# The merge of a two-layer encoder trunk, computed by token with 512 weight columns per product

## The chip, the cores and the metric

The kernel runs on one core of a Trainium2 chip. The metric is the device time of one execution in microseconds. The core has five engines that run side by side: TensorE (PE, matrix products; its weight loads are listed as PEld), VectorE (DVE), ScalarE (ACT), GpSimd (POOL) and SyncE (SP). SP and POOL also issue DMAs.

## What is computed

The reference is a trunk of two layers over 256 tokens of width 1024. A layer normalizes its input, projects it (18688 columns in all), runs three token mixers A, B and C in parallel, and merges them:

```python
for l in range(DEPTH):                      # 2 layers
    h = rmsnorm(x, norm_g[l])
    proj = h @ w_in[l]                      # inputs of all mixers, gates, merge logits
    y_a = hgrn2_mixer(...) * silu(a_g)      # (256, 1024)
    y_b = retention_mixer(...) * silu(b_g)  # (256, 2048)
    y_c = rwkv7_mixer(...) * silu(c_g)      # (256, 1024)
    gates = sigmoid(merge.reshape(b, t, 3, D_MODEL))
    mixed = (gates[:, :, 0] * (y_a @ w_branch_a[l])
             + gates[:, :, 1] * (y_b @ w_branch_b[l])
             + gates[:, :, 2] * (y_c @ w_branch_c[l]))
    x = x + mixed @ w_out[l]
return rmsnorm(x, final_norm_g)
```

All arrays are float32. The merge is the part from `gates` to `x + mixed @ w_out`.

## The kernel before

**Two steps of building.** The kernel first records every operation of all engines (`Plan.note`, L274) with the operations that it depends on and a price (`Plan.cost`, L313). `Plan.order` (L372) then plays the engines against each other with these prices: each engine takes, among the operations whose inputs are there, the one with the lowest rank (60 ns times its number in the record, less the length of the work that hangs on it, `Plan.rank`, L444). `Plan.issue` (L448) emits the instructions in that order; so every instruction of the trace has line L453. Which engine runs what next is thus fixed by the prices and the recorded dependences. `Plan.parts` (L227) gives the parts of a tile that an operation touches, in pieces of 16 columns by 32 partitions. A DMA is priced with a time on the issuing queue, a transfer time by its bytes, and a time to landing.

**Weights.** `load_w` (L527) brings a block of 1024 rows by 256 columns as two halves of 512 KB. Each goes into a raw buffer `w_in` by an SP DMA; ScalarE casts it to `w_hi` (float32r), VectorE subtracts to get `w_lo`. There are three raw buffers, five `w_hi` and four `w_lo` (`RW`, L30). The five inputs of the A mixer (`CCE`, L29) come over the POOL queue instead: one DMA into `w_hi`, a negated copy by ScalarE, and an accumulating DMA into `w_lo`.

**Products.** Every large product is made of three float32r products (high by high, high by low, low by high) for each of eight k tiles. `feat_mm` (L546) has the weights as the stationary operand, 128 columns at a time, and moves the 256 tokens past them; its output is by feature. `tok_mm` (L556) has 128 tokens stationary and moves 256 weight columns; its output is by token. Either way a block takes 48 products that move 256 columns each. Outputs lie in PSUM banks of 512 float32 per partition, named by tag: two "pj", two "c", two "n", one "s", one "ab" (`BANKS`, L116).

**A layer.** The C mixer is prepared (`c_prep`, `c_solve`) and scanned (`c_scan`) in eight pairs of heads; between them run the A pairs and then the B pairs (`FILL`). Their results go to DRAM (ya, yb, yc). Then comes `tail` (L1110), the merge. For each branch m (A, B with two halves of rows, C) and each of four blocks b of 256 columns: a gate product into "pj", its sigmoid as exp, min, ln, exp on ScalarE and VectorE into a tile `t_g` (three buffers, TG), the branch product into two "c" banks, a multiplication, and an addition to the sum `t_acc`. Outputs are by feature, as the output projection needs its stationary operand. With the last branch the sum is cast to `m_hi` and subtracted to `m_lo`. The output projection ("wo") then makes four blocks of 256 columns by token; each is added to x, and the squares are summed for the next norm. `load_y` (L1100) fetches a mixer's result when its branch begins. `norm_T` (L593) makes the next layer's h; `final_norm` (L1156) ends the last layer. Nothing but the planned order parts the merge from the scans: its gate products need h alone, so they may run while the scans do.

In the trace tiles carry the names of their places: "ab_vg_t" is `t_g`, "ab_kq_t" and "ab_c_t" are the sum, "c_wa_t" and "c_qm_t" are `m_hi` and `m_lo`, "c_bd_t" is x, "c_y_t" the squares, "c_W_t" their sums. The branch products read "ab_ex_t" (A), "c_Z_t" (B) and "c_rkvg_t" (C).

Of the kernel before, what the change touches and what calls it, by code (L numbers as in the profile page):

```python
# [19 lines left out]
D = 1024  # L20
T = 256
# [3 lines left out]
TOK = ("ai", "bv", "wo")  # L25
# [38 lines left out]
def _blocks():  # L64
# [8 lines left out]
    for p in range(4):  # L73
        r.append((("bq", p), "w_in", 0, [(5120 + 256 * p, 256)]))
        r.append((("bk", p), "w_in", 0, [(6144 + 256 * p, 256)]))
        for h in (2 * p, 2 * p + 1):
            r.append((("bv", h), "w_in", 0, [(7168 + 256 * h, 256)]))
            r.append((("bg", h), "w_in", 0, [(9216 + 256 * h, 256)]))
    for m in range(3):
        for b in range(4):  # L80
            c = 256 * b
            r.append((("mg", m, b), "w_in", 0, [(15616 + 1024 * m + c, 256)]))
            for n, w, r0 in ((("wa", "w_branch_a", 0),), (("wb0", "w_branch_b", 0), ("wb1", "w_branch_b", 1024)),
                             (("wc", "w_branch_c", 0),))[m]:
                r.append(((n, b), w, r0, [(c, 256)]))
    for b in range(4):
        r.append((("wo", b), "w_out", 0, [(256 * b, 256)]))
# [3 lines left out]
for _i, _b in enumerate(_blocks()):  # L91
    BK[_b[0]] = _i
assert len(BK) == NBLK
# [28 lines left out]
class Plan:  # L122
# [3 lines left out]
    def __init__(self, ctx, tc, some):  # L126
# [4 lines left out]
        self.homes, self.base, self.top, self.place, self.turn, self.psum, self.ndram, self.cache = {}, {}, 0, {}, {}, {}, 0, {}  # L131
        self.last, self.readers, self.bank, self.fill = {}, {}, {}, {}
        self.width, self.tenant, self.before = dict(HOMES), {}, {}
        self.width.update({f"w_{k}{i}": 1024 for k, m in RW.items() for i in range(m)})
        for n, k in BANKS:
            for i in range(k):
                t = self.pp.tile([128, 512], F32, name=f"{n}{i}")[:, :]
                self.psum[n, i] = t
                self.base[t.tensor.name] = (None, f"{n}{i}")
# [3 lines left out]
    def home(self, n, era, dt):  # L143
        old = self.tenant.get(n)
        if old is None or self.tiles[old][1] != era:
            k, w = len(self.tiles), self.width[n]
            if old is not None:
                top, size = self.tiles[old][3], 4 * (w // 16 + 2)
                self.before[k] = {p for g in range(top, top + size) for p in [self.last.get(g, -1)] + self.readers.get(g, [])} - {-1}
            self.tiles.append((n, era, dt, self.top, bass.AP(tensor=self.some.tensor, offset=k << 20, ap=[[w, 128], [1, w]]), w))  # L150
            self.top += 4 * (w // 16 + 2)
# [3 lines left out]
    def real(self, ap):  # L155
# [3 lines left out]
        if k not in self.made:  # L159
            n, era, dt, _, _, w = self.tiles[k]  # L160
# [47 lines left out]
    def dram(self):  # L208
        plan = self

        class Dram:
            def tile(self, shape, dt, name, tag=None):
                plan.ndram += 1
                t = plan.dp.tile(shape, dt, name=f"{name}_{plan.ndram}")[:]
                plan.base[t.tensor.name] = (plan.top, 0)
                plan.top += int(np.prod(shape)) // 32 + 1
# [10 lines left out]
    def parts(self, ap):  # L227

        off = int(ap.offset)
        if ap.tensor.name == self.some.tensor.name:  # L230
            if off < 1 << 20:
                return ()
            _, _, _, base, _, w = self.tiles[off >> 20]
            off &= (1 << 20) - 1
        else:
            b = self.base.get(ap.tensor.name)
            if b is None:
                return ()
            base, w = b
            if base is None:  # L240
                return w
        dims = tuple((int(s), int(c)) for s, c in ap.ap)
        key = (base, off, dims)
        r = self.cache.get(key)
        if r is None:
            if w:
                p, c = divmod(off, w)
                ix = np.array([c])
                for s, n in dims[1:]:
                    if s:  # L250
                        ix = (ix[:, None] + s * np.arange(n)).ravel()
                ix = np.unique(ix // 16)
                r = [base + 4 * int(i) + q for q in range(p // 32, (p + dims[0][1] - 1) // 32 + 1) for i in ix]
            else:
                ix = np.array([off])
                for s, n in dims:
                    if s:
                        ix = np.unique((ix[:, None] + s * np.arange(n)).ravel())
                r = [base + int(i) for i in np.unique(ix // 32)]
            self.cache[key] = r  # L260
        return r
# [12 lines left out]
    def note(self, eng, op, args, kw):  # L274
# [4 lines left out]
        pred, true, rd, wr, fresh = set(), set(), [], [], False  # L279
        for a, w in aps:  # L280
            p = self.parts(a)
            if isinstance(p, str):
                if p in self.bank:
                    pred.add(self.bank[p])
                self.bank[p] = n
            else:
                (wr if w else rd).extend(p)
                if w and (op == "copy_predicated" or "accum_op" in kw):
                    rd.extend(p)
        last, readers = self.last, self.readers  # L290
        for g in rd:
            if g in last:
                true.add(last[g])
        for g in wr:
            if g in last:
                pred.add(last[g])
                pred.update(readers.get(g, ()))
            else:
                fresh = True
        if fresh and out.tensor.name == self.some.tensor.name:  # L300
            pred |= self.before.get(int(out.offset) >> 20, set())
        for g in rd:
            readers.setdefault(g, []).append(n)
        for g in wr:
            last[g] = n
            readers[g] = []
# [6 lines left out]
    def cost(self, eng, op, out, ins, args, kw):  # L313
# [3 lines left out]
        def psum(a):  # L317
            return self.base.get(a.tensor.name, (0,))[0] is None

        both = False  # L320
        if op == "dma_start":
# [50 lines left out]
    def order(self):  # L372
# [26 lines left out]
        use, slow = {}, {0: False}  # L399

# [6 lines left out]
        for _ in range(N):  # L407
# [13 lines left out]
            if e == "tensor":  # L421
# [3 lines left out]
                while x < at + hold:  # L425
# [3 lines left out]
                    x = y  # L429
            start[n], now[e] = at, at + hold  # L430
            moves = o[1] == "dma_start"
            if moves:
                dma = max(at + (700. if e == "sync" else 1500.), dma) + o[6]
                end = dma + 1100. + HOP
            for s in succ[n]:
# [21 lines left out]
def trunk(ctx: ExitStack, tc, x, wb, pp, lora, cst, gtab, ng, out):  # L457
# [68 lines left out]

    def load_w(l, key):  # L527

        W = []
        for h in range(2):  # L530
            src = wb[2 * (l * NBLK + BK[key]) + h]
            hi, lo = plan.weight("hi"), plan.weight("lo")
            if key[0] in CCE or key in CCE:

                G.dma_start(hi, src)
                S.activation(lo, hi.bitcast(F32), AF.Copy, scale=-1.0)
                G.dma_start(lo, src, accum_op=ALU.add)
            else:
                raw = plan.weight("in")
                SY.dma_start(raw, src)  # L540
                S.copy(hi, raw)
                V.tensor_sub(lo, raw, hi.bitcast(F32))
            W.append((hi, lo))
        return W

# [564 lines left out]
    def tail(l, ya, yb, yc, x_src, early, pool):  # L1110
        acc = [early.tile([128, 2, T], F32, name=f"t_acc{b}") for b in range(4)]
        Y, xs = [], None
        for m in range(3):
            br = ((("wa", 0),), (("wb0", 1), ("wb1", 2)), (("wc", 3),))[m]
            for b in range(4):
                o = proj(l, ("mg", m, b))
                g = early.tile([128, 2, T], F32, tag="t_g", bufs=TG, name="t_g")
                S.activation(g, o, AF.Exp, scale=-1.0)
                sigmoid_of_exp(g)
                if b == 0:  # L1120
                    Y += [load_y(src, early, pool if m else early, n) for src, n in (((ya, 0),), ((yb[:, 0:8], 1), (yb[:, 8:16], 2)), ((yc, 3),))[m]]
                o = [ps.tile([128, 256], F32, tag="c", name="t_o") for f in range(2)]
# [173 lines left out]
```

## Time and profile before

| | |
|---|---|
| median of 3 runs | 1712.34 us (1711.75 to 1714.05) |
| the profiled execution | 1706.83 us |
| its span, first to last instruction | 1705.0 us |
| TensorE busy | 1627.3 us (95%) |
| VectorE busy | 1265.2 us (74%) |
| ScalarE busy | 1131.8 us (66%) |
| mean granted clock of TensorE | 0.987 |

The profile is of one execution. Busy time is the union of an engine's instructions. Products are pipelined: the duration shown for one is longer than the distance to the next, so what one costs in a row of them is read from starts. The granted clock is 1.00 at 2.4 GHz and 0.50 at 1.2 GHz. A plain float32 product is recorded as two passes, each with a weight load of its own.

### The profile page before, as it was taken

The numbers are of one execution on the slowest core, as the hardware profiler recorded it, in microseconds if no ns is written. First come the engines' busy times: TensorE is split into PE (matmuls) and PEld (weight loads), VectorE is DVE, ScalarE is ACT, GpSimd is POOL, SyncE is SP. The second block draws the span as 40 slices with busy tenths as digits, with TensorE's granted clock in tenths as the row PEclk, the third lists the DMA queues.
The fourth block names the chain that finished last, engine by engine and source line by source line (L and its number), as shares of the span: only waits on it lengthen the run. The fifth ranks groups of instructions, "written<-read, shape, count | busy, mean of one in ns | idle before, by whom it ended". The sixth has DMA issues, their size and how long they took to land.

```text
span 1705.0 us, 33613 instructions
## 1 busy us (share of the span) xinstructions
PE 1627.3 (95%) x12960; PEld 1594.7 (94%) x12960; DVE 1265.2 (74%) x2613; ACT 1131.8 (66%) x2196; POOL 132.4 (8%) x216
## 2 busy tenths in 40 slices
PE   6989999999999999999998899999999999999997
PEld 6878999999999999999898799998899999999997
DVE  5598889897777986555557888899967878865554
ACT  5877778775756757545559587878657567665553
POOL 1211121100000000000021111220000000000000
PEclk9999999999999999999989899999999999999999
DMA  7968788645455456565568767885454554565653
GB/s 247 233 159 187 173 179 206 142 146 169 120 159 143 124 164 223 177 198 185 189 201 190 174 146 207 198 189 111 134 181 117 171 137 136 169 209 178 199 183 103
DMA packets 139392, 292.24 MB, mean 171 GB/s; under 512 B 63584, under 2 KB 68064, under 8 KB 138976
## 3 DMA queue, kind: packets, MB, share of 16 engines
q1 hardware_dynamic: 116192, 206.20, 39.9%
q0 software_dynamic: 23040, 83.90, 22.0%
q8 instruction: 102, 1.67, 0.4%
q14 instruction: 58, 0.48, 0.1%
HBM read 271.17 MB, written 14.68 MB: 168 GB/s over the span
## 4 chain that ended last, share of the span: by engine, by line
PE 70%; DVE 8%; DMA 8%; issue 7%; ACT 6%; POOL 1%; SPq 1%; DVEq 0%; POOLq 0%; ACTq 0%
PE pj L453 38%; PE c L453 16%; PE n L453 9%; PE ab L453 5%; DMA w_in<-in_wb_dram 2%; PE s L453 2%; DMA w_hi<-in_wb_dram 2%; DVE c_tq L453 2%; DMA ab_ex<-ab_ex 1%; DVE w_lo L453 1%; DVE ab_e L453 1%; ACT c_ux L453 1%; ACT w_hi L453 1%; SPq L453 1%; DVE ab_p L453 1%
## 5 line engine op out<-in xcount | busy, mean ns | idle before, releaser
L453 PE MATMUL pj<-h_hi,w_hi 128*128 128x256 f32 x1952 | 562.3, 297 | 10.3 <-ACT ab_e L453 3.5
L453 PE MATMUL pj<-h_hi,w_lo 128*128 128x256 f32 x1952 | 558.3, 295 | 1.7 <-DMA w_lo<-in_wb_dram 1.0
L453 PE MATMUL pj<-h_lo,w_hi 128*128 128x256 f32 x1952 | 553.5, 292 | 0.1
L453 DVE TENSOR_TENSOR w_lo<-w_in,w_hi 128x1024 fp32r<-128x1024 f32 x292 | 354.3, 1220 | 178.3 <-PE pj L453 47.9
L453 ACT CAST w_hi<-w_in 128x1024 fp32r<-128x1024 f32 x292 | 305.2, 1049 | 206.9 <-PE pj L453 70.0
L453 PEld LDWEIGHTS pj<-h_hi,w_hi 128*128 128x128 f32 x1952 | 369.9, 193 | 14.9 <-ACT ab_e L453 3.7
L453 PEld LDWEIGHTS pj<-h_hi,w_lo 128*128 128x128 f32 x1952 | 369.0, 193 | 4.1 <-DMA w_lo<-in_wb_dram 1.4
L453 PEld LDWEIGHTS pj<-h_lo,w_hi 128*128 128x128 f32 x1952 | 369.8, 193 | 2.2 <-DVE h_lo L453 0.6
L453 PE MATMUL pj<-w_lo,h_hi 128*128 128x256 f32 x384 | 111.6, 291 | 2.7 <-DMA w_lo<-in_wb_dram 2.7
L453 PE MATMUL pj<-w_hi,h_hi 128*128 128x256 f32 x384 | 112.5, 293 | 1.4 <-ACT ab_ex L453 1.4
L453 PE MATMUL c<-c_Z,c_bd 128*128 128x192 f32 (+1 forms) x512 | 106.3, 309 | 7.6 <-ACT c_bd L453 4.6
L453 PE MATMUL pj<-w_hi,h_lo 128*128 128x256 f32 x384 | 110.5, 288 | 0.0
L453 PE MATMUL c<-c_Z_t,w_hi 128*128 128x256 f32 x512 | 95.7, 284 | 0.0
L453 ACT COPY c_y<-n 128x128 f32<-128x128 f32 (+1 forms) x160 | 61.8, 392 | 45.8 <-PE n L453 43.7
L453 PEld LDWEIGHTS c<-c_Z,c_bd 128*128 128x128 f32 x512 | 80.6, 196 | 10.2 <-ACT c_bd L453 6.6
L453 ACT ACTIVATE w_lo<-w_hi 128x1024 fp32r<-128x1024 f32 x80 | 84.4, 1056 | 7.7 <-DMA w_hi<-in_wb_dram 5.6
L453 POOL DMA_DIRECT2D w_lo<-in_wb_dram x80 | 71.2, 891 | 175.8 <-ACT w_lo L453 76.2
L453 PE MATMUL n<-c_y,c_wa 128*128 128x128 f32 x512 | 81.1, 279 | 2.5 <-ACT c_y L453 1.5
L453 DVE TENSOR_TENSOR c_tq<-c_W,c_M 128x16 f32<-128x16 f32 (+6 forms) x112 | 81.9, 732 | 1.4
L453 PE MATMUL ab<-ab_e 128*128 128x128 f32 x448 | 73.7, 286 | 8.3 <-DVE ab_p L453 2.5
L453 PEld LDWEIGHTS c<-c_Z_t,w_hi 128*128 128x128 f32 x512 | 79.0, 190 | 0.2
L453 PEld LDWEIGHTS pj<-w_lo,h_hi 128*128 128x128 f32 x384 | 73.3, 191 | 3.8 <-DMA w_lo<-in_wb_dram 3.4
(195 smaller groups left out, 3604.9 us busy)
## 6 DMA issues: line engine op xcount, KB each, us to landing
w_in<-in_wb_dram SPq DMA_DIRECT2D x292, 512.0 KB, 3.8
w_hi<-in_wb_dram POOLq DMA_DIRECT2D x80, 512.0 KB, 5.4
w_lo<-in_wb_dram POOLq DMA_DIRECT2D x80, 512.0 KB, 7.1
c_M<-s SPq DMA_DIRECT2D x64, 128.0 KB, 5.0
c_ux<-in_lora_dram SPq DMA_DIRECT2D x16, 256.0 KB, 2.8
ab_e<-in_gtab_dram SPq DMA_DIRECT2D x16, 256.0 KB, 2.7
ab_ex<-ab_ex SPq DMA_DIRECT2D x16, 256.0 KB, 5.5
yb<-ab_e SPq DMA_DIRECT2D x16, 256.0 KB, 4.0
```

The costliest lines, as they stand in the source:

```text
L453: getattr(getattr(self.tc.nc, eng), op)(*map(self.real, args), **{k: self.real(v) for k, v in kw.items()})
```

## The change

The merge's blocks become 512 columns wide (`WIDE`): per branch two instead of four, and two for the output projection. `wide_mm` has 128 tokens of h, y or m stationary and moves 512 weight columns; a pair of PSUM banks, one per 128 tokens, is filled side by side, k tile by k tile, each half block of 512 KB serving two k tiles. Gates and sums are now by token. After the last branch each sum tile (128 tokens by 512 features) is transposed on TensorE in four pieces into an "n" bank, from which `m_hi` and `m_lo` are taken. The weights are packed on the host to match.

The record keeps, for each tile, exact masks of columns (still by 32 partitions) with the operations that last wrote and read them. Prices change: a POOL DMA holds its queue for 550 ns (870 if it accumulates) instead of 1000 and lands later, a queue is taken to have at most eight DMAs in flight, and for plain float32 products the width of the stationary operand counts in place of that of the moving one.

```diff
-TOK = ("ai", "bv", "wo")
+TOK = ("ai", "bv")
+WIDE = ("mg", "wa", "wb0", "wb1", "wc", "wo")
...
     for m in range(3):
-        for b in range(4):
+        for b in range(2):
+            r.append((("mg", m, b), "w_in", 0, [(15616 + 1024 * m + 512 * b, 512)]))
...
-                ix = np.unique(ix // 16)
+            flag = np.zeros(int(ix[-1]) + 1, np.uint8)
+            flag[ix] = 1
+            r = m = int.from_bytes(np.packbits(flag, bitorder="little").tobytes(), "little")
...
+            if not w or op == "copy_predicated" or "accum_op" in kw:
+                true.update(p for x, p in wrote if x & m)
+            if w:
+                pred.update(p for x, p in wrote if x & m)
+                pred.update(p for x, p in read if x & m)
...
-            return (380. if eng == "sync" else 1000.), b / (330. if run >= 512 else 330. * max(run, 64) / 512), both
+            return (380. if eng == "sync" else 870. if "accum_op" in kw else 550.), b / (330. if run >= 512 else 330. * max(run, 64) / 512), both
...
-            n, m = size(out), size(ins[-1])
+            n, m = size(out), size(ins[0])
...
-                return (1800. if a[0] == "sync" else 2600.) + a[6] + HOP
+                return (1800. if a[0] == "sync" else 3300.) + a[6] + HOP
...
+            if moves and len(land[e]) >= SLOTS:
+                at = max(at, land[e][-SLOTS] + HOP)
...
-                dma = max(at + (700. if e == "sync" else 1500.), dma) + o[6]
+                dma = max(at + (700. if e == "sync" else 2200.), dma) + o[6]
...
+    def wide_mm(l, key, o, h, first=True, last=True):
+        hhi, hlo = h
+        for k in range(KT):
+            if k % 2 == 0:
+                whi, wlo = (w.rearrange("p (k c) -> p k c", c=512) for w in load_half(l, key, k // 2))
+            for t in range(2):
+                r = slice(128 * t, 128 * t + 128)
+                for i, (a, b) in enumerate(((hhi, whi), (hlo, whi), (hhi, wlo))):
+                    PE.matmul(o[t], a[:, k, r], b[:, k % 2], start=(first and k == 0 and i == 0),
+                              stop=(last and k == KT - 1 and i == 2))
...
-        acc = [early.tile([128, 2, T], F32, name=f"t_acc{b}") for b in range(4)]
+        acc = [early.tile([128, 512], F32, name=f"t_acc{i}") for i in range(4)]
...
-                o = proj(l, ("mg", m, b))
+                o = [ps.tile([128, 512], F32, tag="pj") for t in range(2)]
+                wide_mm(l, ("mg", m, b), o, (h_hi, h_lo))
...
+                o = [ps.tile([128, 512], F32, tag="c") for t in range(2)]
                 for i, (key, y) in enumerate(br):
-                    W = load_w(l, (key, b))
-                    for f in range(2):
-                        feat_mm(o[f], W, f, Y[y], first=(i == 0), last=(i == len(br) - 1))
+                    wide_mm(l, (key, b), o, Y[y], first=(i == 0), last=(i == len(br) - 1))
...
+                for t in range(2):
+                    s = acc[2 * t + b]
+                    V.tensor_mul(gs[t] if m else s, o[t], gs[t])
+                    if m:
+                        V.tensor_add(s, s, gs[t])
+                    if m == 2:
+                        x = ps.tile([128, 4, 128], F32, tag="n", name="t_t")
+                        for k in range(4):
+                            PE.transpose(x[:, k], s[:, 128 * k:128 * k + 128], ident)
+                        r = m_hi[:, 4 * b:4 * b + 4, 128 * t:128 * t + 128]
+                        S.copy(r, x)
+                        V.tensor_sub(m_lo[:, 4 * b:4 * b + 4, 128 * t:128 * t + 128], x, r.bitcast(F32))
...
-        for b in range(4):
-            W = load_w(l, ("wo", b))
+        for b in range(2):
+            o = [ps.tile([128, 512], F32, tag="c" if b else "pj") for t in range(2)]
+            wide_mm(l, ("wo", b), o, (m_hi, m_lo))
```

## Rows read from the trace of the kernel before

**Rows 1.** The page: busy us, share of the span and instructions by engine.

```profile
PE 1627.3 (95%) x12960; PEld 1594.7 (94%) x12960; DVE 1265.2 (74%) x2613; ACT 1131.8 (66%) x2196; POOL 132.4 (8%) x216
```

**Rows 2.** Stretches: length, busy PE, PEld, DVE, ACT, POOL, PEclk, DMA share, GB/s.

```profile
60.00:160.00 100.00, 87.96 (x652) 83.21 (x651) 83.05 (x210) 75.51 (x152) 18.82 (x29) 0.97 0.83 189
866.00:980.00 114.00, 100.18 (x730) 95.96 (x729) 81.55 (x195) 80.38 (x165) 21.61 (x33) 0.94 0.77 192
1140.00:1210.00 70.00, 66.35 (x510) 64.03 (x508) 63.05 (x149) 54.26 (x117) 6.87 (x11) 0.98 0.60 151
210.00:300.00 90.00, 90.00 (x739) 88.86 (x738) 76.39 (x187) 72.11 (x155) 16.89 (x25) 1.00 0.85 193
980.00:1060.00 80.00, 79.44 (x663) 78.72 (x661) 68.74 (x174) 64.72 (x134) 14.83 (x23) 1.00 0.77 184
600.00:716.00 116.00, 115.61 (x959) 114.39 (x958) 79.03 (x132) 73.79 (x128) 0.16 (x1) 1.00 0.62 193
716.00:846.00 130.00, 130.00 (x1085) 129.84 (x1084) 73.68 (x92) 66.31 (x85) 0.00 (x0) 1.00 0.57 182
1564.00:1696.00 132.00, 132.00 (x1100) 131.71 (x1099) 72.49 (x90) 64.03 (x85) 0.00 (x0) 1.00 0.50 161
857.70:859.50 1.80, 1.80 (x10) 1.80 (x10) 0.14 (x1) 0.00 (x0) 0.52 (x2) 0.50 0.41 137
```

**Rows 3.** The chain that ended last: start us, length us, what.

```profile
733.03 10.24 PE c L453 x86
...
1673.04 23.05 PE pj L453 x192
```

**Rows 4.** Timeline of PE at half clock, ten rows alike: start us, us, instruction.

```profile
857.41 0.41 PE L453 MATMUL pj<-h_hi,w_lo 128*128 128x256 f32 x1
...
859.33 0.41 PE L453 MATMUL pj<-h_hi,w_lo 128*128 128x256 f32 x1
```

**Rows 5.** Timeline of plain f32 passes (PE) and of weight loads (PEld).

```profile
1256.85 1.89 PE L453 MATMUL ab<-ab_vg,ab_p 128*128 128x256 f32 x8
...
887.74 0.38 PE L453 MATMUL c<-c_rkvg,c_ux 128*128 128x256 f32 x1
...
171.63 0.75 PEld L453 LDWEIGHTS s<-c_y 128*128 128x128 f32 x6
172.30 0.19 PEld L453 LDWEIGHTS pj<-w_hi,h_lo 128*128 128x128 f32 x1
```

**Rows 6.** Timeline of PE around four transposes of the scan.

```profile
616.01 0.60 PE L453 MATMUL n<-cst,c_bd 128*128 128x128 f32 x4
616.37 0.36 PE L453 MATMUL pj<-w_lo,h_hi 128*128 128x256 f32 x1
```

**Rows 7.** Groups of ACT and DVE, 716 to 846 us: busy, mean ns, idle before.

```profile
L453 ACT CAST w_hi<-w_in 128x1024 fp32r<-128x1024 f32 x44 | 46.1, 1050 | 47.8 <-PE c L453 29.8 <-PE pj L453 13.4 <-DMA w_in<-in_wb_dram 3.8
L453 ACT ACTIVATE ab_vg_t<-ab_vg_t 128x512 f32<-128x512 f32 x15 | 9.5, 631 | 1.6 <-DVE ab_vg_t L453 1.0
L453 ACT CAST c_wa_t<-ab_kq_t 128x512 fp32r<-128x512 f32 x3 | 1.9, 619 | 2.0 <-DVE ab_kq_t L453 2.0
...
L453 DVE TENSOR_TENSOR w_lo<-w_in,w_hi 128x1024 fp32r<-128x1024 f32 x44 | 53.7, 1222 | 39.8 <-issue 12.6 <-PE c L453 11.9 <-ACT ab_vg_t L453 7.7
L453 DVE TENSOR_TENSOR ab_kq_t<-ab_kq_t,ab_vg_t 128x512 f32<-128x512 f32 x6 | 4.1, 690 | 0.1
```

**Rows 8.** The chain after the last output product: start us, length us, what.

```profile
1696.11 0.43 DVE c_bd_t L453
...
1697.57 0.17 DVE c_W_t L453
```

**Rows 9.** DMA issues (KB, median us to landing), and POOL's group of accumulating loads.

```profile
w_in<-in_wb_dram SPq DMA_DIRECT2D x292, 512.0 KB, 3.8
w_lo<-in_wb_dram POOLq DMA_DIRECT2D x80, 512.0 KB, 7.1
...
L453 POOL DMA_DIRECT2D w_lo<-in_wb_dram x80 | 71.2, 891 | 175.8 <-ACT w_lo L453 76.2 <-ACT c_y L453 24.3 <-ACT c_bd L453 14.3
```

More of the change, by code (lines that the diff above doesn't have):

```diff
@@ L147, in home @@
             if old is not None:
[L148 to L151, printed above, removed]
+                self.before[k] = {p for x in self.live.get(old, ()) for _, p in x}
+            self.tiles.append((n, era, dt, w, bass.AP(tensor=self.some.tensor, offset=k << 20, ap=[[w, 128], [1, w]])))
             self.tenant[n] = k
@@ L278, in note @@
         out, ins = aps[0][0], [a for a, w in aps if not w]
-        pred, true, rd, wr, fresh = set(), set(), [], [], False
+        pred, true, acc = set(), set(), []
         for a, w in aps:
[L281 to L306, printed above, removed]
+            where, m = self.parts(a)
+            if where is None:
+                continue
+            if not m:
+                if where in self.bank:
+                    pred.add(self.bank[where])
+                self.bank[where] = n
+                continue
+            acc.append((where, m, w))
+            wrote, read = self.live.setdefault(where, ([], []))
+            if not w or op == "copy_predicated" or "accum_op" in kw:
+                true.update(p for x, p in wrote if x & m)
+            if w:
+                pred.update(p for x, p in wrote if x & m)
+                pred.update(p for x, p in read if x & m)
+                if m & ~self.covered.get(where, 0):
+                    pred |= self.before.get(where, set())
+        for where, m, w in acc:
+            wrote, read = self.live[where]
+            if w:
+                wrote[:] = [(x & ~m, p) for x, p in wrote if x & ~m]
+                read[:] = [(x & ~m, p) for x, p in read if x & ~m]
+                self.covered[where] = self.covered.get(where, 0) | m
+        for where, m, w in acc:
+            self.live[where][0 if w else 1].append((m, n))
         true = {p for p in true if self.ops[p][0] != eng or eng != "tensor"}
@@ L317, in psum @@
         def psum(a):
[L318 removed]
+            return self.base.get(a.tensor.name, 0) is None
         both = False
@@ L399, in order @@
         use, slow = {}, {0: False}
+        SLOTS, land = 8, {e: [] for e in ENGINES}
         def halved(w):
@@ L524, in trunk, with load_half @@
     V.tensor_scalar(omlb, lb, -1.0, 1.0, op0=ALU.mult, op1=ALU.add)
-    def load_w(l, key):
[L529 to L544, printed above, removed]
+    def load_half(l, key, h):
+        src = wb[2 * (l * NBLK + BK[key]) + h]
+        hi, lo = plan.weight("hi"), plan.weight("lo")
+        if key[0] in CCE:
+            G.dma_start(hi, src)
+            S.activation(lo, hi.bitcast(F32), AF.Copy, scale=-1.0)
+            G.dma_start(lo, src, accum_op=ALU.add)
+        else:
+            raw = plan.weight("in")
+            SY.dma_start(raw, src)
+            S.copy(hi, raw)
+            V.tensor_sub(lo, raw, hi.bitcast(F32))
+        return hi, lo
+    def load_w(l, key):
+        return [load_half(l, key, h) for h in range(2)]
+    def wide_mm(l, key, o, h, first=True, last=True):
[8 more added lines that the diff above has]
+                              stop=(last and k == KT - 1 and i == 2))
     def feat_mm(o, W, f, h, first=True, last=True):
@@ L1140, in tail @@
+        s4 = pool.tile([128, 2, 2], F32, name="t_s4")
         ss = pool.tile([128, 2], F32, name="t_ss")
```

117 lines of the change are left out of this document (56 added, 61 removed).

## The prediction

> **What bounds the kernel now.** I read the page first: TensorE is busy for 1627.3 of the 1705.0 us span, VectorE for 74%, ScalarE for 66% [rows 1]. A busy share is an average, so the second view is the table of stretches [rows 2]. The reader should see three kinds. In the merge (716 to 846 us, 1564 to 1696 us) TensorE is busy in every microsecond at a granted clock of 1.00, VectorE and ScalarE are not: TensorE alone sets the time there. In the stretches where the A blocks come in over the POOL queue (60 to 160, 866 to 980, 1140 to 1210 us) it idles for 29.5 us together. In 210 to 300 and 980 to 1060 us, which hold the same kind of work, it idles for 0.6. Third, the chain of work that ended last: in the merge it is nothing but matmuls, 86 branch products in 10.24 us and the 192 of an output projection in 23.05, that is 0.119 and 0.120 us for one f32r product of 256 columns [rows 3].
>
> **What one product costs, and why.** At full clock (2.4 GHz) 256 columns at one per cycle would stream in 0.107 us, so 0.013 of the 0.120 is something else. Three views say what. Just after the layer boundary the granted clock is 0.50 (1.2 GHz) [rows 2] and the first and the last of ten such products start 1.92 us apart, 0.213 a step [rows 4]: 256 cycles of 1.2 GHz and nothing added. So the 0.013 is hardly a fixed charge per instruction. Plain f32 products, whose passes stream one column per cycle of 1.2 GHz, show the other half [rows 5]: eight passes of 256 columns take 1.89 us, less the 0.38 that a last one shows until its end is 1.51 for seven starts, 0.216 each, 0.003 above the stream; and six weight loads for products of only 64 columns begin within 0.67 us, 0.112 each, though such a product streams in half of that. Each product loads its own 128 columns of weights while the one before it streams. A load takes some 0.11 to 0.12; whichever is longer counts. At 256 columns and full clock the load is the longer one (0.120 against 0.107). At 512 columns the stream (0.213) covers it, so I take 0.216, the f32 pass that also streams for 0.213 under a hidden load. The trace has no f32r product of 512 columns, so the ends are kept: 0.213 (the bare stream) and 0.240 (twice today's, no gain at all), with 0.226 between them (0.013 per instruction after all).
>
> **The change, part by part.** *Products.* Per layer the merge has 12 gate, 16 branch and 4 output blocks of 48 products: 32 x 48 = 1536, in both layers 3072, at 0.120 makes 368.6 us. After it, half as many at 0.216: 1536 x 0.216 = 331.8. Gain 36.8; at the ends 41.4 and 0, in the middle 21.5. All of it lies on the path where rows 2 show TensorE at 100%.
>
> The Trainium skill ("TensorE: Matmul & The Clock Gate", Back-to-back issue gap) gives a sustained 131 ns for a 512-column product among weight loads. By it 1536 products would take an estimated 201 us. The trace speaks against it: 512 columns at twice the rate of rows 4 cannot stream in under 0.213.
>
> *Transposes.* New on TensorE: per layer 2 halves x 2 token tiles x 4 = 16, in all 32. Four of the scan's transposes take 0.44 us (from 616.01 to the next product's end, 616.73, less that product's own 0.28) [rows 6], 0.11 each: 32 x 0.11 = +3.5 us.
>
> The same page (Part 4: PE-mode transpose) puts a transpose at about 275 ns in a kernel's context. With it the term would be an estimated 8.8 us. Rows 6 show that as the length of one, not as the distance between two.
>
> *Handover from merge to output projection.* Today the last block's sum reaches m_lo while the projection works through the k tiles of earlier blocks. Now half of k hangs on the last pair: multiply 0.69, add 0.69 on VectorE, four transposes 0.44, a cast 0.62 and a subtraction as long as the add [rows 7] make 3.1 us for the first token tile, and the second comes 1.4 later, 4.5 in all, some 5 with the steps between engines. TensorE meanwhile has the first half of k: 24 products, 5.2 us. That cover is thin; one weight subtraction of 1.22 us in VectorE's queue ahead of it breaks it. Ends 0 and 2.5 per layer; I take 1, so +2. Behind the waiting transposes on TensorE stand only output products; the products of the next half block, if their weights are there, may be ordered ahead.
>
> *End of a layer.* The closing add goes from 256 to 512 columns (0.43 [rows 8] to 0.69), the square by about as much to 0.63 [rows 7], but the first token tile ends three products, 0.65 us, ahead of the second: +0.2 a layer, +0.4. Now this end takes 1.46 us from 1696.11 to the reduction at 1697.57.
>
> *Feeding.* A 512 KB half block of weights is used up in 12 x 0.216 = 2.59 us instead of 24 x 0.120 = 2.88. It costs ScalarE 1.05 and VectorE 1.22 [rows 7]. Between 716 and 846 us ScalarE waited ahead of its 44 casts 43.2 us for TensorE to free a buffer, 0.98 per cast, and 3.8 for the DMA [rows 7]; 0.29 less per half block leaves 0.69 spare. So at nothing, as long as that spare time is there. Bytes, sigmoids and gates stay as many. PSUM: a pair of outputs now takes both "pj" or both "c" banks, but gate and branch products alternate, so a pair is read out (two 0.63 us activations) while the other tag has 10 us of products.
>
> *The order.* Exact columns, new prices for POOL DMAs, a limit of eight in flight and weight loads in the price of narrow f32 products redraw the whole order, A stretches too. The POOL issue price of an accumulating load (0.87 for 1.0) is nearer to the trace (0.891 [rows 9]), and a narrow product is now priced by its two loads, as rows 5 have it. Nothing in the trace shows a new order. Bounds: all 29.5 us of idle in the A stretches go, or the clean stretches of 170 us fall to the 10% of the bad ones (29.5 in 284 us), +17.7. I take -3, nearer to nothing than to either end, and +-10 as its likely part.
>
> **Sum.** -36.8 + 3.5 + 2 + 0.4 - 3 = -33.9 us. Against the profiled execution (1706.83 us, of which 1705.0 is the span) that is 1672.9. The median of the shown runs is 1712.34, 5.5 above that execution; the range and the prediction stand on the median: 1678.4.
>
> **Rivals.** (1) A charge of 0.013 stays per instruction: 1693.7. The 0.213 at half clock speaks against it. 0.10.
> (2) Columns are the limit at full clock (0.240): all but the products' gain remains, 1715.2, no difference. Against it: the f32 passes; for it: no full-clock row streams faster than 256 columns in 0.12. 0.04.
> (3) The gate and branch products of the first branch fill TensorE while the last scans run (to about 716 us). If the scans then end no earlier, the quarter of the gain that is made there (8 of 32 blocks, 9.2 us) turns into idle time: 1687.6. TensorE idles for 0.39 in 600 to 716 us now [rows 2], so the filler is just enough. 0.06.
> (4) Slower: the weights don't come in time. There are three raw buffers, each held for landing 3.8 + cast 1.05 + subtraction 1.22 = 6.1 us [rows 7, 9], one half block per 2.0 us. It decides from 7.8 us on (2.59 x 3), and above 8.6 it is slower than today. With landings of 7.1, as the accumulating loads have under load [rows 9], it is 9.4, or 3.12 per half block: 128 x (3.12 - 2.88) = +31, about 1746. DMA engines at 0.57 in the merge [rows 2] speak against it. 0.03.
> (5) Slower: the new order loses more than the products win, over 37 us of new stalls in the A stretches, twice today's; with +45 it is 1726. 0.05.
> (6) The skill's 131 ns: 1712.3 - 168 + 3 = 1547. 0.01.
>
> **How the numbers follow.** The forecast has 0.71. Its own range is 1664 to 1693: order +-10, handover 0 to 5, a product at 0.213 to 0.217. The range of 8 in 10 takes in rivals 1 and 3: 1660 to 1697. A difference of 0.2%, 3.4 us, is about what can be told from none here. Faster by more: the forecast with rivals 1, 3 and 6: 0.88. Within: rival 2, 0.04. Slower: rivals 4 and 5, 0.08.
>
> **What would show it.** In the merge, starts 0.216 apart for 512 columns (0.226: rival 1; 0.240: rival 2). The merge from its first branch-B product to the end of the output projection shorter by a tenth, with TensorE still at 100%. Idle at the first output projection's second half of k under 2.5 us. ScalarE still waiting for TensorE, not for the DMA, ahead of its casts (else rival 4). Idle in the A stretches within 20 and 40 us together (else the order term is wrong). The forecast is wrong if a 512-column product takes over 0.23 us, or if the stretches before the merge lose what it wins.

## The result and the profile after

| | before | after |
|---|---|---|
| time, median (us) | 1712.05 | 1684.49 |
| lowest and highest (us) | 1710.78 to 1714.05 | 1684.01 to 1685.98 |
| profiled execution (us), its span | 1706.83, 1705.0 | 1684.01, 1682.2 |

After over before is 0.9839, 95% interval 0.9822 to 0.9856: 27.6 us faster. The forecast was 1678.4, range 1660 to 1697. So the direction and the range held, and the point was 6.1 too low. Behind that stand two terms that were off by more than that, in opposite directions; that the point came as near as it did is luck.

The page of after, in the columns of [rows 1]: TensorE issues 1504 instructions fewer (1536 products less, 32 transposes more), and its busy time falls by 17.1 us, not by the 33 of the forecast's products and transposes. VectorE, ScalarE and POOL do what they did.

```profile
PE 1610.2 (96%) x11456; PEld 1512.9 (90%) x11456; DVE 1262.9 (75%) x2581; ACT 1128.5 (67%) x2180; POOL 133.0 (8%) x216
```

The table of stretches of after, with the columns of [rows 2]; the first three are the ones in which the A blocks come in over the POOL queue, the last three lie in the merges, 820 to 840 us around the place where the first merge hands over to its output projection:

```profile
60.00:160.00 100.00, 89.70 (x662) 87.25 (x662) 78.13 (x205) 76.51 (x161) 19.06 (x29) 0.91 0.80 179
866.00:980.00 114.00, 103.82 (x778) 100.01 (x777) 84.58 (x204) 86.50 (x173) 23.90 (x37) 0.96 0.85 205
1140.00:1210.00 70.00, 65.26 (x511) 62.56 (x511) 64.69 (x159) 55.71 (x117) 4.06 (x7) 1.00 0.54 132
...
700.00:820.00 120.00, 119.58 (x555) 99.47 (x554) 68.19 (x75) 62.28 (x81) 0.00 (x0) 1.00 0.61 191
820.00:840.00 20.00, 20.00 (x92) 16.38 (x91) 12.09 (x14) 8.09 (x13) 0.00 (x0) 1.00 0.54 168
1540.00:1670.00 130.00, 130.00 (x604) 107.96 (x603) 71.73 (x79) 63.74 (x86) 0.00 (x0) 1.00 0.55 172
```

The merge is still TensorE alone, at a granted clock of 1.00. The second number in a row is the one to read: 130.00 of 130. The weight loads (third number) now leave 17 to 18% of the time free, where they filled it before (129.84 of 130 [rows 2]). The chain of waits (start us, length us, what) then gives the price of one product:

```profile
744.86 7.71 PE pj L460 x34
752.56 21.94 PE c L460 x96
...
1664.55 8.06 PE c L460 x35
1672.64 0.70 DVE c_bd_t L460
1673.42 1.34 ACT c_y_t L460 x4
1674.79 0.17 DVE c_W_t L460
```

7.71 / 34 is 0.227, 21.94 / 96 is 0.2285, 8.06 / 35 is 0.230. The forecast had 0.216.

### The profile page after: what moved, and what is told of

Read it like the earlier page. It is cut to its first block, busy times and chain, and to the rows that moved or that the text cites. A ratio compares the mean times of both kernels' runs of the same rounds, so it can differ in the third digit from the quotient of the medians.

```text
span 1682.2 us, 30624 instructions
## 1 busy us (share of the span) xinstructions
PE 1610.2 (96%) x11456; PEld 1512.9 (90%) x11456; DVE 1262.9 (75%) x2581; ACT 1128.5 (67%) x2180; POOL 133.0 (8%) x216
## 4 chain that ended last, share of the span: by engine, by line
PE 67%; DVE 12%; issue 8%; DMA 7%; ACT 5%; POOL 1%; DVEq 0%; SPq 0%; POOLq 0%; ACTq 0%
PE pj L460 35%; PE c L460 15%; PE n L460 9%; PE ab L460 5%; DMA w_in<-in_wb_dram 3%; DVE w_lo L460 2%; DVE ab_e L460 2%; DMA w_lo<-in_wb_dram 2%; PE s L460 2%; DVE c_tq L460 1%; DVE c_Z L460 1%; DVE ab_p L460 1%; ACT w_hi L460 1%; DMA w_hi<-in_wb_dram 1%; DVE c_ux L460 1%
## 5 line engine op out<-in xcount | busy, mean ns | idle before, releaser
L460 PE MATMUL pj<-h_hi,w_hi 128*128 128x256 f32 x1568 | 457.7, 300 | 7.2 <-DVE ab_kq L460 2.2
L460 PE MATMUL pj<-h_hi,w_lo 128*128 128x256 f32 x1568 | 453.7, 298 | 2.0 <-DMA w_lo<-in_wb_dram 1.5
L460 PE MATMUL pj<-h_lo,w_hi 128*128 128x256 f32 x1568 | 450.6, 295 | 1.3 <-DVE h_lo L460 1.3
L460 PEld LDWEIGHTS pj<-h_lo,w_hi 128*128 128x128 f32 x1568 | 297.4, 193 | 2.8 <-DVE h_lo L460 1.8
L460 PE MATMUL pj<-w_lo,h_hi 128*128 128x256 f32 (+1 forms) x576 | 176.4, 331 | 4.1 <-DMA w_lo<-in_wb_dram 3.7
L460 PE MATMUL pj<-w_hi,h_hi 128*128 128x256 f32 (+1 forms) x576 | 178.6, 334 | 1.3 <-ACT ab_ex L460 1.3
L460 PE MATMUL pj<-w_hi,h_lo 128*128 128x256 f32 (+1 forms) x576 | 174.7, 328 | 0.0
L460 PEld LDWEIGHTS pj<-w_hi,h_hi 128*128 128x128 f32 x576 | 110.8, 193 | 8.8 <-ACT ab_ex L460 1.5
L460 PEld LDWEIGHTS pj<-w_hi,h_lo 128*128 128x128 f32 x576 | 110.7, 193 | 7.3
L460 PE MATMUL c<-c_Z,c_bd 128*128 128x128 f32 (+1 forms) x512 | 105.6, 304 | 6.9 <-ACT c_bd L460 5.7
L460 PEld LDWEIGHTS c<-c_Z,c_bd 128*128 128x128 f32 x512 | 79.1, 192 | 10.3 <-ACT c_bd L460 7.2
L460 PE MATMUL ab<-ab_e 128*128 128x128 f32 x448 | 73.5, 286 | 11.9 <-DVE ab_e L460 8.2
```

The costliest lines, as they stand in the source:

```text
L460: getattr(getattr(self.tc.nc, eng), op)(*map(self.real, args), **{k: self.real(v) for k, v in kw.items()})
```

## The experiments

Three theories stood against each other. By the first, which is the prediction's, a wide product costs 0.216 and the rest is the order. By the second, rival 1 of the prediction, a charge of 0.013 stays on each product at full clock. By the third, the merge's new shape has little to do with it and the gain comes from the redrawn order.

### What one product costs

`probe` is the kernel after with products appended behind its end; nothing reads what they compute.

```diff
+        def run(cols, rows=128, dt=F32R, two=False, same=False, n=32):
...
+            for i in range(n):
...
+                pe.matmul(o[i // 3 % 2 if two else 0][0:rows, 0:cols], w[:, k:k + rows], a[:, 512:512 + cols], start=True, stop=True)
+        run(512, n=64)
+        run(384)
+        run(256)
+        run(128)
+        run(512, rows=64)
+        run(256, rows=64)
+        run(512, two=True)
+        run(512, same=True)
+        run(512, dt=BF)
+        run(256, dt=BF)
+        run(512, dt=F32, n=12)
```

> The changed kernel with a row of extra products behind its last work on TensorE (their results are not used): float32r products of 512, 384, 256 and 128 moved columns with 128 stationary columns; 512 and 256 with only 64 stationary columns; 512 into two banks in turn; 512 with the same weights each time; bfloat16 products of 512 and 256; plain float32 of 512. Theory F (a fixed charge per float32r product at full clock, beside the stream): starts 0.227 apart for 512, 0.173 for 384, 0.120 for 256, and the same with 64 stationary columns. Theory L (the recorded one, mended: the rest of a weight load shows in every product): with 64 stationary columns half of the charge, 0.220 and 0.113. If the charge goes with four-byte operands, bfloat16 products of 512 come 0.216 apart, else 0.227. Two banks or the same weights change nothing under either. Plain float32: two passes of 0.429 under both.

The timeline of PE in the probe (start us, length us, instruction). The first two lines are 34 products apart; of the other groups the first recorded product is shown, 32 of a kind in each (31 of the wide bf16 ones, whose first has no record; an f32 line, x2, is one product in two passes). A product's own length is latency, so read the starts. The last two lines are weight loads (PEld), of float32r and of bf16 products:

```profile
1679.11 0.39 PE L474 MATMUL c<-h_hi,h_lo 128*128 128x512 f32 x1
...
1686.81 0.39 PE L474 MATMUL c<-h_hi,h_lo 128*128 128x512 f32 x1
1687.04 0.33 PE L474 MATMUL c<-h_hi 128*128 128x384 f32 x1
...
1692.61 0.28 PE L474 MATMUL c<-h_hi 128*128 128x256 f32 x1
...
1696.44 0.22 PE L474 MATMUL c<-h_hi 128*128 128x128 f32 x1
...
1699.96 0.39 PE L474 MATMUL c<-h_hi 128*64 128x512 f32 x1
...
1707.33 0.28 PE L474 MATMUL c<-h_hi 128*64 128x256 f32 x1
...
1710.97 0.40 PE L474 MATMUL c<-h_hi 128*128 128x512 f32 x1
...
1725.73 0.38 PE L474 MATMUL c<-h_hi,h_lo 128*128 128x512 bf16 x1
...
1732.42 0.27 PE L474 MATMUL c<-h_hi 128*128 128x256 bf16 x1
...
1735.91 1.02 PE L474 MATMUL c<-h_hi 128*128 128x512 f32 x2
1736.77 1.02 PE L474 MATMUL c<-h_hi,h_lo 128*128 128x512 f32 x2
...
1699.79 0.19 PEld L474 LDWEIGHTS c<-h_hi,h_lo 128*128 128x128 f32 x1
...
1732.97 0.10 PEld L474 LDWEIGHTS <-h_hi 128*128 128x128 bf16 x1
```

Differences over counts, all at full clock:

| operands | columns | weight columns | apart (us) | columns / 2.4 GHz |
|---|---|---|---|---|
| float32r | 512 | 128 | 0.227 | 0.213 |
| float32r | 384 | 128 | 0.174 | 0.160 |
| float32r | 256 | 128 | 0.120 | 0.107 |
| float32r | 128 | 128 | 0.110 | 0.053 |
| float32r | 512 | 64 | 0.230 | 0.213 |
| float32r | 256 | 64 | 0.114 | 0.107 |
| bf16 | 512 | 128 | 0.216 | 0.213 |
| bf16 | 256 | 128 | 0.109 | 0.107 |
| plain f32, one pass | 512 | 128 | 0.429 | (1.2 GHz) 0.427 |

This settles the price, though not what causes it. From 256 to 512 columns a float32r product costs its stream and 0.013 to 0.014 more, the same at all three widths. Bf16 products and plain f32 passes pay 0.002 to 0.003. Sums in two banks by turns and the same weights each time (0.227 apart both), which ran between these groups, change nothing; with the same weights the 32 loads are recorded all the same. So each float32r product, taken with its weight load, bears a charge at full clock, and at half clock it is not seen [rows 4]. Bf16 changes the product and the load at once (a load's record is 0.10 long for 0.19), so the two are not told apart. Only at 128 columns does the weight load (0.112 [rows 5]) set the distance. That the 0.120 at 256 columns sits just above the load's 0.112 is then mostly a coincidence of two numbers, as the charge is the same at 384 and 512, and the prediction took it for the cause. A product with 64 weight columns at 256 takes 0.114, which the mended theory L expected (0.113): with half the weights to load, part of the charge is gone. At 512 it takes 0.230, where theory L expected 0.220 and theory F 0.227. Why that is so stays open.

The Trainium skill ("TensorE: Matmul & The Clock Gate", "Wait — 56ns, not 53.3ns?") tells of a fixed cost of about 2.5 ns per product that shows at full clock only. The bf16 rows agree (215.8 by its formula, 216 measured). The float32r rows have the same shape, with 13 ns in its place.

`split` is the kernel after with each wide product that neither opens nor closes a sum issued as two products of 256 columns, 1424 more in all; order and all else as in after.

```diff
+                if op == "matmul" and len(args[2].shape) == 2 and args[2].dtype == F32R and args[2].shape[1] == 512 and not (kw["start"] or kw["stop"]):
+                    for c in (slice(0, 256), slice(256, 512)):
+                        self.tc.nc.tensor.matmul(self.real(args[0])[:, c], self.real(args[1]), self.real(args[2])[:, c], **kw)
+                    continue
```

> The changed kernel in the same order of instructions, but each merge product of 512 columns that neither opens nor closes a bank is issued as two of 256 (1424 more products in all). It keeps everything of the change but the width. Theory F: 1424 x 0.0133 = +19 us, 1703.5. Rival (what the width brings is small, and the gain is the order's): within 4 us of the changed kernel, 1684 to 1688.

Measured: 1694.78 us, 10.3 above after (0.9894 of before, 0.9871 to 0.9917). Neither expectation held: the theory's +19 was too much, the rival's 4 too little. The chain of waits in its second merge, and the line of after from which the same blocks start there:

```profile
1579.64 0.46 PE pj L464 x2
1580.10 10.54 PE pj L462 x88
1590.64 0.47 PE pj L464 x2
...
1591.57 21.85 PE c L462 x184
...
1683.96 0.70 DVE c_bd_t L464
```

```profile
1572.52 10.89 PE pj L460 x48
```

184 products in 21.85 us are 0.1188 each, two are 0.2375, and one wide product in its place was 0.2285: 1424 x 0.009 = 12.8 us by these rows. Other blocks lose more: 48 gate products take 10.89 in after and 0.46 + 10.54 + 0.47 = 11.47 here, 0.013 for each of the 44 split ones. Over the nine blocks of 48 up to the last add (1572.52 to 1672.64 in after, 1579.64 to 1683.96 here) 400 split products cost 4.20 us, 0.0105 each, which makes 15.0 for 1424. The probe's prices (twice 0.120 for 0.227) would make it 18.5, the forecast's 34. The kernel gave up 10.3. So the width of the products, in an order held fixed, is worth 10 us by the kernel's time and 13 to 15 by its rows. That is all that halving their number buys here.

### The merge, the record and the prices, each alone

The diff holds three things that can be had apart: the merge by token, the exact record of operands, and the prices with the limit in flight. All combinations were run.

```diff
# merge: blocks of 512 columns, wide_mm, tail; record and prices as before
+TOK = ("ai", "bv")
+WIDE = ("mg", "wa", "wb0", "wb1", "wc", "wo")
# masks: operands recorded to the column; merge and prices as before
+            flag = np.zeros(int(ix[-1]) + 1, np.uint8)
+            flag[ix] = 1
...
+                pred.update(p for x, p in wrote if x & m)
+                pred.update(p for x, p in read if x & m)
# prices: issue prices, landing lags, eight in flight, weight loads; merge and record as before
+            return (380. if eng == "sync" else 870. if "accum_op" in kw else 550.), b / (330. if run >= 512 else 330. * max(run, 64) / 512), both
```

`merge`:

> The kernel before with the new merge alone (512 columns, transposes), the record by 16 columns and the prices as they were. Theory: -17.0 by count of products, 1695. Rival (the merge's form is what frees the rest): 1685.

`masks`:

> The kernel before with the exact record of columns alone; prices and merge as they were. Theory M (dependences that the pieces of 16 columns invented held the order back): most of the 19 us that record and prices gave together, 1693 to 1698. Theory P (the prices did it): 1709 to 1714.

`prices`:

> The kernel before with the new prices alone (POOL DMAs, eight in flight, width of the stationary operand); record and merge as they were. Theory P: 1693 to 1698. Theory M: 1709 to 1714. Theory N (any redrawn order falls somewhere, neither part carries it): both of this and the one with the record alone away from the sum, or one of them slower than before.

`planner` (masks and prices, the old merge):

> The kernel before with the new record (exact columns) and the new prices, its merge as it was (by feature, 256 columns). Theory: TensorE's work per layer is 8.5 us less in the changed kernel by count of products, 17.0 in all, so the remaining 10.6 of the 27.6 us are the order's: 1701.5. Rival (the order alone brings nothing, the new merge loosens the schedule around it): 1712.

`merge_masks`:

> The changed kernel with the old prices. Theory M: within 4 us of the changed kernel, 1681 to 1689. Theory P: as the new merge alone, 1703 to 1709. Theory N: away from both.

`merge_prices`:

> The changed kernel with the old record by 16 columns. Theory P: 1681 to 1689. Theory M: as the new merge alone, 1703 to 1709. Theory N: away from both.

| merge | record | prices | kernel | median (us) | ratio to before |
|---|---|---|---|---|---|
| old | old | new | prices | 1704.65 | 0.9967 (0.9948 to 0.9986) |
| old | exact | old | masks | 1689.60 | 0.9874 (0.9840 to 0.9908) |
| old | exact | new | planner | 1692.58 | 0.9897 (0.9861 to 0.9933) |
| wide | old | old | merge | 1707.27 | 0.9977 (0.9958 to 0.9995) |
| wide | old | new | merge_prices | 1693.82 | 0.9901 (0.9866 to 0.9936) |
| wide | exact | old | merge_masks | 1685.78 | 0.9848 (0.9812 to 0.9884) |
| wide | exact | new | after | 1684.49 | 0.9839 (0.9822 to 0.9856) |

Each part's worth is read by the four pairs that differ in it alone, by differences of medians (before lay at 1711.8 beside planner and merge, at 1710.5 beside the other four). The exact record: -21, -12, -21.5, -9. The wide merge: -4.5, -4, -11, -8. The prices: -6, +3, -13.5, -1. The record alone gives 1689.6; with it in place, the merge and the prices together add another 5. Had the products brought most of the gain, as the forecast has it, merge would lie near after and masks near before. It is the other way round. The expectations fared badly. In planner and merge both that were written down were missed, by 9 and 12 us at the nearest. Theory M (the record) held in merge_masks, and masks came out 3 us below its range. In prices and merge_prices the time lies between the ranges of M and P, as theory N has it: the order's worth doesn't add up from its parts.

Where the record's gain lies is seen in the two layers' lengths. The table of stretches, one row for each layer (its end is that of its last output product): first before, then masks, merge, and after.

```profile
0.00:847.80 847.80, 810.27 (x6480) 793.64 (x6480) 632.26 (x1300) 568.17 (x1097) 66.26 (x110) 1.00 0.64 176
847.80:1696.00 848.20, 816.96 (x6481) 801.04 (x6480) 629.57 (x1309) 561.86 (x1091) 66.16 (x106) 0.98 0.61 168
```

```profile
0.00:843.20 843.20, 809.03 (x6480) 793.46 (x6480) 628.78 (x1300) 568.78 (x1097) 66.93 (x110) 1.00 0.63 176
843.20:1678.30 835.10, 809.62 (x6481) 793.24 (x6480) 629.22 (x1309) 564.35 (x1092) 66.51 (x106) 0.99 0.62 170
```

```profile
0.00:846.40 846.40, 806.63 (x5728) 756.90 (x5728) 631.07 (x1285) 564.58 (x1089) 66.07 (x110) 0.99 0.65 176
846.40:1700.10 853.70, 812.70 (x5729) 760.36 (x5728) 631.52 (x1294) 561.98 (x1084) 67.05 (x106) 0.99 0.62 166
```

```profile
0.00:841.80 841.80, 806.68 (x5728) 758.68 (x5728) 629.03 (x1284) 565.90 (x1088) 67.06 (x111) 0.99 0.65 177
841.80:1672.60 830.80, 803.28 (x5729) 754.19 (x5728) 629.91 (x1293) 560.56 (x1084) 65.92 (x106) 0.99 0.63 171
```

Take the second number from the first: TensorE's idle time is 37.5 + 31.2 = 68.7 us before, 34.2 + 25.5 = 59.7 with the exact record alone, 39.8 + 41.0 = 80.8 with the wide merge alone, 35.1 + 27.5 = 62.6 after. Busy time falls by 8.5 with the record though its products are the same ones. A product at half clock counts as busy for longer (0.213 for 0.120, [rows 4]), and the mean granted clock of the second layer rises from 0.98 to 0.99. The sums of the stretches in which the granted clock is 0.50, without the first 25 us, before and with the record:

```profile
sum 40.80, PE 36.11; mean PE 5.16
```

```profile
sum 27.30, PE 23.44; mean PE 4.69
```

That is 12.7 us less of busy time at half clock, and at 0.213 for 0.120 it makes some 5.5 of the 8.5. By these rows about half of the record's gain is waiting that is gone, and about a third is TensorE running at full clock for more of the time; the remaining 3 us are not traced. The wide merge alone shows the opposite: 12.1 us more idle time takes back what its products win. Part of the 12.1 is chance: the profiled execution of merge (1710.97) lies 3.7 above its median, that of before 5.5 below. Its list of TensorE's waits (us in total, times, longest) names two that grew; in before the first is 3.7 and the second is not in the list, which goes down to 2.3:

```profile
PE pj L457 <- DMA w_lo<-in_wb_dram: 9.8, 9, 2.9
...
PE n L457 <- DMA c_wa<-s: 4.7, 2, 4.4
```

None of that lies in the merge: 6.4 of the first and 4.4 of the second fall between 850 and 1200 us, in the mixers, which the edit doesn't touch. It is the order that was redrawn.

Which of the recorded dependences matter was not tried. Between before and masks 1307 of 100236 are gone from the plan, 466 of them between engines, most around the 4-column steps of the C mixer's triangular solve, the batch statistics and small scalars, which the old record put into common pieces of 16 columns. Of the 1307, 977 still follow from other dependences, so that only 330 (120 between engines) cease to bind; 5911 are new, and each of them followed from the old ones already. So few loosened ties moved the time by more than a change of rank does.

### How much an order is worth by itself

To see how far a redraw with no purpose moves a kernel, the weight of an operation's place in the program, in the rank that the order is drawn by, was changed a little, in before and in after.

```diff
-        return [60. * n - d for n, d in enumerate(depth)]
+        return [57. * n - d for n, d in enumerate(depth)]
```

> The kernel before with one number of its planner changed: rank 57 instead of 60 ns per number in the record. Nothing of record, prices or merge changes; only the order is drawn anew. Theory D (the order's 21 us are mostly one draw against another): redrawn orders of the kernel before spread by 10 us or more, some near 1695. Theory M (the exact record frees the order): within 5 us of 1711.

> The same with 63 ns. Theory D: away from 1711 by 10 us or more in this or the former. Theory M: 1706 to 1716.

> The changed kernel with rank 57 instead of 60 ns. Theory D: away from 1684.5 by 10 us or more in this or the next, up as likely as down. Theory M: within 5 us, 1680 to 1690.

> The changed kernel with 63 ns. Theory D: as the former. Theory M: 1680 to 1690.

| weight | before (us) | ratio | after (us) | ratio |
|---|---|---|---|---|
| 57 | 1704.98 | 0.9959 (0.9930 to 0.9988) | 1679.39 | 0.9822 (0.9763 to 0.9880) |
| 63 | 1711.37 | 0.9991 (0.9968 to 1.0014) | 1688.83 | 0.9865 (0.9818 to 0.9912) |

Before lay at 1713.3 beside these, after is taken at its 1684.5. Theory D wanted 10 us or more and got it nowhere; theory M's 5 us held at 63, and at 57 was missed by 1 in before and after. Such a redraw moves a kernel by 8.3 us down to 4.3 up. That bounds what the table of parts can carry. Between two redraws of one kernel there can then be some 9 us (after, from 57 to 63: 9.4). The exact record moves all four pairs the same way, by 9 to 21, three of them by more than that. Taken together, six orders were drawn with the old record (before with 57, 60 and 63, prices, merge, merge_prices) and took 1693.8 to 1713.3; the six with the exact one (masks, planner, merge_masks, after with 57, 60 and 63) took 1679.4 to 1692.6, with no overlap. That it helps is shown, its size only roughly. The prices, of both signs, are not told apart from a redraw. The wide merge by itself (4 to 11) would not be either; its worth rests on probe and split, where the order is held. The fastest of all, after with 57, overlaps after and is not claimed as better.

## Why the prediction was right, and where it was wrong

**The bound.** Right. The merge was and is TensorE alone, so what a product costs there is paid in full.

**The price of a wide product.** This is the step that failed. "So the 0.013 is hardly a fixed charge per instruction" was concluded from the half-clock rows, where nothing is added [rows 4]. The probe shows that the charge exists at full clock only. The row was read rightly and carried over to a clock for which it says nothing. The value taken, 0.216, came from f32 passes [rows 5], another type of product. The chain gives 0.227 to 0.230 in its place. At 0.2285 the products' term is 368.6 - 1536 x 0.2285 = 17.6 us, not 36.8; by split's rows it is 1536 x 0.0105 = 16.1, and by split's time 11. Rival 1, held at one chance in ten, had the charge and, with 21.5, was nearer to the size.

**Transposes.** Right. The chain of after has single ones at 0.11 us (at 821.31 and 821.65), and the timeline of PE one of them and three in a row:

```profile
821.15 0.27 PE L460 MATMUL n<-cst,ab_kq_t 128*128 128x128 f32 x1
...
822.16 0.49 PE L460 MATMUL n<-cst,ab_c_t 128*128 128x128 f32 x3
```

One alone has a length of 0.27 us, three together 0.49: 0.11 for each one more. Together with the products that is a net gain of 8 to 14 us, against 33.3 forecast.

**Handover.** Taken as +2, measured as nothing: TensorE is busy for 20.00 of 20.00 us around it, and in the second layer 130.00 of 130. The reason is in the order: of the 24 products of the first half of k, 12 run ahead of the last transposes and 12 behind them. The timelines show VectorE's last two subtractions into m_lo and the first products of the second half of k:

```profile
823.66 1.29 DVE L460 TENSOR_TENSOR c_qm_t<-n,c_wa_t 128x512 fp32r<-128x512 f32 x2
...
825.26 0.63 PE L460 MATMUL pj<-w_hi,c_wa_t 128*128 128x512 f32 x2
```

The subtractions end at 824.95, and TensorE gets there at 825.26, 0.31 later. The cover was as thin as the prediction said, and it held.

**End of a layer.** Taken as +0.4, and about +2.5. The last end takes 2.15 us from the add to the reduction (1672.64 to 1674.79) for 1.46 [rows 8], and between the layers TensorE idles for 5.87 us instead of 4.11. The squares were priced alone. The timeline of ACT in after shows what stands ahead of them:

```profile
842.49 1.04 ACT L460 CAST w_hi<-w_in 128x1024 fp32r<-128x1024 f32 x1 [1.78 <-DMA w_in<-in_wb_dram]
843.44 0.62 ACT L460 ACTIVATE c_y_t<-c_bd_t 128x512 f32<-128x512 f32 x1
...
844.07 1.03 ACT L460 CAST w_hi<-w_in 128x1024 fp32r<-128x1024 f32 x1
845.00 0.62 ACT L460 ACTIVATE c_y_t<-c_bd_t 128x512 f32<-128x512 f32 x1
```

Both adds are done by 843.2, but two casts of the next layer's weights (1.04 and 1.03) stand ahead of one square each, and the second square ends at 845.6. The step left out what else is queued on the engine that it moves work on. At the last end no cast stands there, and it is still 0.69 longer: the last products of the two token tiles start 0.23 apart (1672.20 and 1672.44), not three products as forecast, so that the second tile's add and square come right behind the first's.

**Feeding.** No time was lost, but the sign that was to show it came out the other way. The groups of ACT and DVE from 700 to 820 us in after:

```profile
L460 ACT CAST w_hi<-w_in 128x1024 fp32r<-128x1024 f32 x41 | 43.1, 1052 | 50.5 <-DMA w_in<-in_wb_dram 39.1 <-PE c L460 5.7 <-PE pj L460 3.3
...
L460 DVE TENSOR_TENSOR w_lo<-w_in,w_hi 128x1024 fp32r<-128x1024 f32 x41 | 50.1, 1223 | 40.8 <-PE c L460 24.3 <-PE pj L460 9.0 <-issue 5.2
```

The waits of SP's DMA queue in the same stretch (us in total, times, longest):

```profile
SPq L460 <- DVE w_lo L460: 98.2, 41, 7.5
```

Ahead of its casts ScalarE now waits 39.1 us for the DMA, against 3.8 before [rows 7], and only 9.0 for TensorE. By the prediction's last part that is rival 4. But TensorE idles for 0.42 in those 120 us. The waits have changed places: VectorE's subtractions wait 33.3 us for TensorE to free a buffer (11.9 for its "c" products before [rows 7]), the raw buffers come free late, so their loads start late (SP's queue waits 98.2 us for those subtractions), and ScalarE sees a late load. The loop is still paced by TensorE; a wait for a DMA is the last link of it. The sign that decides is whether TensorE waits.

**Filler.** Rival 3 didn't happen at the size that it was given. The stretches of after in which the last scans run, with the columns of [rows 2]:

```profile
600.00:700.00 100.00, 97.59 (x635) 88.41 (x635) 70.34 (x119) 66.77 (x114) 0.16 (x1) 1.00 0.60 190
...
1430.00:1540.00 110.00, 108.20 (x690) 97.36 (x689) 77.56 (x126) 70.86 (x118) 0.16 (x1) 1.00 0.62 192
```

TensorE idles for 2.41 and 1.80 us there, against 0.39 in 600 to 716 us before [rows 2], and for 0.42 in 700 to 820. So at most some 4 of its 9.2 were lost.

**The order.** The second mis-sized term. "Nothing in the trace shows a new order" was true, and -3 +-10 was too narrow on the side of a gain: the exact record moved the kernel by -9 to -21. The bound at that end was the idle time of the A stretches, 29.5 us. That idle time fell only to 25.2 (284.00 less 258.78, rows above), and the layers' idle time by 6.1; the rest came in part as full clock, which the bound left out (TensorE is busy for 26.7 us at a granted clock of 0.50 after the first 25 us, against 36.1 before), and from places outside those stretches. The forecast of 20 to 40 us for them held.

**The signs.** The starts in the merge came out 0.227 to 0.230 apart, at the edge of the 0.23 that was named as the end of the forecast; two products of 0.120 turned into one of 0.2285 are a twentieth less, not a tenth.

**The sum.** With -11 to -18 for the products, +3.5, 0 for the handover and +2.5 for the ends, the parts that have a place make -5 to -12. The medians fell by 27.6, which leaves -16 to -23; the two profiled executions differ by 22.8 (before's lay 5.5 under its median), which leaves -11 to -18. That remainder goes to the order. It is what is left, not measured by itself, and it fits the record's -9 to -21. So the products gave less than half of what was forecast, and the order four to eight times as much. One error of 19 to 26 us and one of 8 to 20 went opposite ways, and the time came out near the forecast by luck. The range held with less of it: it had been drawn wide enough for rival 1.

## What to carry to other kernels

A price read at one clock, or from another type of product, says nothing of the one that is added: where the trace has no such instruction at the clock that counts, keep the ends apart and give each its full chance. When a kernel's order is drawn by a program, an edit anywhere redraws it everywhere, so measure by how much a redraw without purpose moves the time (here 2 to 8 us) before a part of that size is put down to a cause, and hold the order still to price an instruction. Dependences recorded too coarsely cost time in places that no row names: the exact record was worth about as much here as halving 3072 products, or more.

## What the runs showed of the hardware

- A float32r product pays 0.013 to 0.014 us beside its stream at full clock (0.120, 0.174, 0.227 for 256, 384, 512 columns). Bf16 pays 0.003 (0.216 at 512), a plain f32 pass 0.002 to 0.003 (0.429). At half clock a float32r product of 256 columns takes 0.213, with nothing added.
- At 128 columns a float32r product with 128 weight columns takes 0.110, about the time of a weight load (0.112 [rows 5]), and at 256 columns with 64 weight columns 0.114. At 512 columns with 64 weight columns it takes 0.230, not less than with 128. No run here explains that last one, nor whether the charge is the product's or its weight load's.
